# FFN-up products: wide and narrow matmuls alternate singly, with the narrow product of the low weights ahead of the wide product of the high weights

## The chip, the cores and the metric

The kernel runs on one core of a Trainium2 chip. The metric is the device time of one execution in microseconds. Three timed runs of the kernel before gave 1171.59, 1171.27 and 1169.43 us, so its median is 1171.27 us. The profiled execution, from which all durations below come, took 1171.33 us; its trace spans 1169.3 us from the first to the last instruction. The remaining 2.0 us lie around the span.

## What is computed

The reference is one layer of a decoder trunk on 256 tokens of width 2048: a normalisation, a mixing stage (causal pooling beside an RWKV-7 time mixer) with its output projection, a squared-ReLU feed-forward stage, a gated embedding, and a last normalisation. The feed-forward stage is the one that matters here:

```python
h2 = rms_norm(x, mlp_norm[i])
x = x + jnp.square(jax.nn.relu(h2 @ w_ffn_up[i])) @ w_ffn_down[i]
```

`h2` is 256 x 2048, `w_ffn_up` is 2048 x 8192, `w_ffn_down` is 8192 x 2048, all in float32. The first product, `h2 @ w_ffn_up`, is called FFN-up below, the second FFN-down.

## The kernel before

**Splitting.** Every large product is made of reduced-precision matmuls. Each operand is split into a high part (a rounded copy) and a low part (what the rounding left), and three partial products are added: high by high, low weights by high activations, high weights by low activations. ScalarE writes the high part of the weights (`wh`, L171, two instructions for each block of 1024 columns), VectorE subtracts it from the loaded block to get the low part (`wl`, L172, one instruction). `split_w` does both.

**FFN-up.** `gemm_wide` makes 512 columns of the product at a time, in two halves of 256 columns (each half is one `bank` tile of two PSUM banks, one for each 128 columns, `ct` = 0 and 1). It is called 16 times, so there are 32 halves. A half loads four blocks `raw` of `w_ffn_up`, 128 x 1024 each; a block holds four 128-deep steps `k` of the contraction, 256 columns each. So a half has 16 steps `k`.

Each step `k` is four matmuls, called a *round* below. For both `ct` a **wide** product takes the high weights as the stationary operand and streams 512 columns: the high and the low activations of all 256 tokens side by side (`hl`, two runs of 256). Its first 256 output columns collect high by high, its last 256 high weights by low activations. For both `ct` a **narrow** product takes the low weights and streams the 256 columns of the high activations; it adds into the first 256 output columns of the same bank. Before the change the round is wide, wide, narrow, narrow (L1134 twice, then L1139 twice). There are 32 x 16 = 512 rounds, with 1024 wide and 1024 narrow products.

After the 16th step `consume` is called (`square` in `ffn_half`): ScalarE copies the last 256 columns of both banks out (L1409), VectorE adds the first 256 (L1410), squares the positive part (L1411), and the result is split again for FFN-down. There are two `bank` tiles (pool `psw`), used in turn.

**FFN-down and the rest.** `ffn_half` runs eight calls of `gemm_wide` and then two sweeps over `w_ffn_down` (L1229, 512-column products), and is called twice. So FFN-up has two stretches, about 376 to 556 us and 718 to 896 us. Beside FFN-up, `sums_ahead` prepares sums of `w_ffn_down` blocks (`ta`, L1218 to L1223) on VectorE and writes them to memory.

**What sets the order.** In this part of the kernel no order is written out by hand: a scheduler orders each engine's instructions from the program's text, its priorities (splits of weights have a high one) and the buffers. Loads are issued by SyncE's queue in that order. Loaded blocks have six buffers, high parts five, low parts four. A buffer is free when its last reader is done: the VectorE subtraction for a loaded block, the last wide product of a block for its high part, the last narrow product for its low part.

Of the kernel before, what the change touches and what calls it, by code (L numbers as in the profile page):

```python
# [16 lines left out]
T = 256  # L17
# [23 lines left out]
def trunk(  # L41
# [19 lines left out]
    nc = tc.nc  # L61
# [99 lines left out]
    def load_raw(src, n, name):  # L161
        raw = ring("raw", F32, f"raw_{name}")
        nc.sync.dma_start(raw[:, 0:n], src)
        return raw

    def split_w(raw, name):

        wh, wl = ring("wh", F32R, f"wh_{name}"), ring("wl", F32R, f"wl_{name}")
        with tc.high_priority(20000):
            for a in range(2):  # L170
                nc.scalar.activation(wh[:, a * 512 : (a + 1) * 512], raw[:, a * 512 : (a + 1) * 512], AF.Copy)  # L171
            nc.vector.tensor_tensor(wl, raw, wh.bitcast(F32), op=ALU.subtract)  # L172
        return [(t_h, t_l) for t_h, t_l in zip((wh[:, 0:512], wh[:, 512:1024]), (wl[:, 0:512], wl[:, 512:1024]))]
# [233 lines left out]
    for tt in range(2):  # L407
        for i, q in enumerate((1, 3)):
            nc.tensor.matmul(
                sbank[:, tt : tt + 1], sums[q][:, 0, tt * 128 : (tt + 1) * 128], ones[:, 0:1],  # L410
                start=i == 0 and tt == 0, stop=i == 1, skip_group_check=True,
# [705 lines left out]
    def wide_bank(name):  # L1117
        return psw.tile([128, 2, 512], F32, tag="wide", name=name)

    def gemm_wide(src, acts, name, consume):  # L1120

        for half in range(2):
            bank = wide_bank(f"{name}_w{half}")
            for kq in range(4):
                raw = load_raw(src[half, kq].rearrange("p a n -> p (a n)"), 1024, f"{name}{half}_{kq}")
                for a, (wh, wl) in enumerate(split_w(raw, f"{name}{half}_{kq}")):
                    for b in range(2):
                        k = kq * 4 + 2 * a + b  # L1130
                        hl = acts(k)
                        cs = [slice(b * 256 + ct * 128, b * 256 + ct * 128 + 128) for ct in range(2)]
                        for ct, c in enumerate(cs):
                            nc.tensor.matmul(  # L1134
                                bank[:, ct, :].rearrange("p (s t) -> p s t", s=2), wh[:, c], hl,
                                start=k == 0, stop=False, skip_group_check=True,
                            )
                        for ct, c in enumerate(cs):
                            nc.tensor.matmul(  # L1139
                                bank[:, ct, 0:T], wl[:, c], hl[:, 0, :], start=False, stop=k == 15, skip_group_check=True  # L1140
                            )
            consume(half, bank)

# [257 lines left out]
    def ffn_half(hf):  # L1401
        acts = []
        for i in range(8):
            f = hf * 8 + i

            def square(bi, bank):
                r = fp.tile([128, 512], F32, tag="r", name=f"r{f}_{bi}")
                r2 = r.rearrange("p (c t) -> p c t", c=2)
                nc.scalar.activation(r2, bank[:, :, T : 2 * T], AF.Copy)  # L1409
                nc.vector.tensor_tensor(r2, bank[:, :, 0:T], r2, op=ALU.add)  # L1410
                nc.vector.scalar_tensor_tensor(r, r, 0.0, r, op0=ALU.max, op1=ALU.mult)  # L1411
                pr = i * 2 + bi
                if pr in SEVEN:
                    acts.append(square_seven(r, pr))
                else:
                    acts.append(square_plain(r, pr))

            gemm_wide(w_up[f], h2, f"u{f}", square)
            if f == 1:
                inv_ms()  # L1420
                x_store(1)
            sums_ahead(hf, i // 4, AHEAD[i % 4])

        for j in range(2):
            np_ = (hf + j) % 2
            hooks = {3: lambda: (x_store(1 - np_), x_load(3, np_))} if j else {}
            if hf and j:
                hooks[max(AHEAD) + 1] = lambda: (x_load(4, 1), ps_.extend(split_p()))
            sweep(w_down[:, hf * 16 : hf * 16 + 16], acts, hf, np_, f"d{hf}{np_}", scaled_residual, hooks)
# [163 lines left out]
```

## Time and profile before

| what | value |
|---|---|
| median of three timed runs | 1171.27 us |
| profiled execution | 1171.33 us |
| its span | 1169.3 us |
| FFN-up, two stretches | about 376 to 556 us, 718 to 896 us |
| wide products (L1134) | 1024, recorded at 395 ns on average |
| narrow products (L1139) | 1024, recorded at 278 ns on average |
| low parts of FFN-up weights (L172, `wl_u`) | 128, 1221 ns each |
| high parts of FFN-up weights (L171, `wh_u`) | 256, 624 ns each |

PE stands for the matmuls of TensorE, PEld for its loads of stationary operands, DVE for VectorE, ACT for ScalarE, SP for the queue that issues the loads. A row of a group gives its line, engine, operation, the tile written and the tiles read, the shapes, the number of instructions, then the busy time in us, the mean ns of one, and the time for which the engine was idle just before them with what ended it. Matmuls overlap: the recorded duration of one is longer than the distance to the start of the next, and that distance, called the *pitch* here, is what the time is made of.

### The profile page before, as it was taken

Reading aid. Unit: us, or ns where it says so; the run is one execution under the profiler, and the core shown is the slowest. Engines: PE = TensorE matmul, PEld = TensorE weight load, DVE = VectorE, ACT = ScalarE, POOL = GpSimd, SP = SyncE. Lnnn points to the kernel's source line nnn. Section 1 sums busy time; section 2 is a strip of 40 time slices with the busy share of each in tenths; the row PEclk is TensorE's granted clock in tenths of the full one; section 3 lists DMA queues with packets and bytes.
Section 4 is the critical chain, followed back from the end, with each engine's and each line's share of the span. In section 5 each row is a group of like instructions: output and inputs, shape, how many; then the busy total and the mean of one; then the engine's idle time right before and its main releaser. Section 6 shows DMA issues by size and latency. Waiting matters only on the chain.

```text
span 1169.3 us, 19239 instructions
## 1 busy us (share of the span) xinstructions
PE 1155.1 (99%) x7360; PEld 992.7 (85%) x7360; DVE 904.5 (77%) x1193; ACT 685.9 (59%) x1216; POOL 18.3 (2%) x77
## 2 busy tenths in 40 slices
PE   9999999999999999999999999999999999999997
PEld 8999998787888888888888888888888888888886
DVE  7886898356555787887989988777878899898843
ACT  5868555666545555554764664554555664659733
POOL 4100000000000000000000000000000000000000
PEclk9999999999999999999999999999999999999998
DMA  7554444444756888788677867887986777886812
GB/s 272 163 171 129 156 154 146 138 152 127 233 183 207 303 294 302 260 288 291 219 272 237 304 243 233 302 292 261 323 300 229 264 274 258 292 292 219 302 55 72
DMA packets 73547, 269.36 MB, mean 230 GB/s; under 512 B 8176, under 2 KB 9200, under 8 KB 70512
## 3 DMA queue, kind: packets, MB, share of 16 engines
q1 hardware_dynamic: 73168, 267.78, 66.4%
q8 instruction: 57, 0.93, 0.3%
q10 hardware_dynamic: 288, 0.37, 0.1%
q14 instruction: 34, 0.28, 0.1%
HBM read 246.09 MB, written 22.02 MB: 229 GB/s over the span
## 4 chain that ended last, share of the span: by engine, by line
PE 95%; ACT 2%; DVE 2%; DMA 1%; issue 0%; SPq 0%; DVEq 0%; ACTq 0%
PE u_w L1134 20%; PE d_p L1229 16%; PE u_w L1139 10%; PE d_w L1229 8%; PE d_d L1229 3%; PE o_b L193 2%; PE o_b L194 2%; PE o_b L195 2%; PE gt_b L195 2%; PE gt_b L194 2%; PE gt_b L193 2%; PE zr_b L184 1%; PE zk_b L184 1%; PE zk_b L185 1%; PE zr_b L185 1%; PE zk_b L186 1%
## 5 line engine op out<-in xcount | busy, mean ns | idle before, releaser
L1134 PE MATMUL u_w<-h,wh_u 128*128 128x512 f32 x1024 | 321.7, 395 | 0.0
L171 ACT ACTIVATE wh_u<-raw_u 128x512 fp32r<-128x512 f32 x256 | 147.3, 624 | 152.6 <-PE u_w L1134 94.7
L1139 PEld LDWEIGHTS u_w<-h,wl_u 128*128 128x128 f32 x1024 | 192.3, 188 | 45.3
L1139 PE MATMUL u_w<-h,wl_u 128*128 128x256 f32 x1024 | 201.5, 278 | 0.0
L172 DVE TENSOR_TENSOR wl_u<-raw_u,wh_u 128x1024 fp32r<-128x1024 f32 x128 | 156.1, 1221 | 45.5 <-PE u_w L1139 34.9
L1134 PEld LDWEIGHTS u_w<-h,wh_u 128*128 128x128 f32 x1024 | 156.0, 189 | 0.1
L1229 PE MATMUL d_p<-wh_d,yd 128*128 128x512 f32 x336 | 89.8, 389 | 0.0
L1229 PEld LDWEIGHTS d_p<-wh_d,yd 128*128 128x128 f32 x336 | 62.9, 188 | 12.9
L1291 ACT ACTIVATE th_d<-raw_d 128x1024 fp32r<-128x1024 f32 x40 | 40.3, 1052 | 55.4 <-DVE raw_d L1287 55.4
L171 ACT ACTIVATE wh_d<-raw_d 128x512 fp32r<-128x512 f32 x112 | 63.9, 621 | 9.9 <-ACT th_d L1291 4.8
L172 DVE TENSOR_TENSOR wl_d<-raw_d,wh_d 128x1024 fp32r<-128x1024 f32 x56 | 66.0, 1218 | 0.6 <-PE u_w L1139 0.6
L172 DVE TENSOR_TENSOR wl_o<-raw_o,wh_o 128x1024 fp32r<-128x1024 f32 x32 | 39.1, 1223 | 34.5 <-PE o_b L195 20.6
L171 ACT ACTIVATE wh_o<-raw_o 128x512 fp32r<-128x512 f32 x64 | 36.7, 625 | 39.4 <-PE o_b L194 22.1
L1229 PE MATMUL d_w<-th_d,ys 128*128 128x512 f32 x216 | 55.1, 390 | 0.1
L1293 DVE TENSOR_TENSOR tl_d<-raw_d,th_d 128x1024 fp32r<-128x1024 f32 x40 | 47.3, 1220 | 7.4 <-ACT th_d L1291 7.4
L1229 PE MATMUL d_p<-wl_d,yd 128*128 128x512 f32 x168 | 51.7, 389 | 0.0
L1280 ACT ACTIVATE w7h_d<-raw_d 128x1024 fp32r<-128x1024 f32 x36 | 38.0, 1060 | 22.1 <-PE d_d L1229 11.2
L1293 DVE TENSOR_TENSOR tl_d<-tr_d,th_d 128x1024 fp32r<-128x1024 f32 x32 | 37.8, 1221 | 13.9 <-ACT th_d L1291 13.9
L1229 PEld LDWEIGHTS d_w<-th_d,ys 128*128 128x128 f32 x216 | 40.4, 188 | 9.1 <-ACT th_d L1291 0.8
L1282 DVE TENSOR_TENSOR w7l_d<-raw_d,w7h_d 128x1024 fp32r<-128x1024 f32 x36 | 43.9, 1218 | 3.3 <-PE u_w L1139 1.6
L1229 PE MATMUL d_p<-w7h_d,ys 128*128 128x512 f32 x144 | 44.3, 389 | 0.0
L1291 ACT ACTIVATE th_d<-tr_d 128x1024 fp32r<-128x1024 f32 x32 | 32.2, 1052 | 11.8 <-PE d_p L1229 11.7
(393 smaller groups left out, 2650.1 us busy)
## 6 DMA issues: line engine op xcount, KB each, us to landing
raw_u<-in_w_ffn_up_dram SPq DMA_DIRECT2D x128, 512.0 KB, 5.9
raw_d<-in_w_ffn_down_dram SPq DMA_DIRECT2D x112, 512.0 KB, 5.0
raw_o<-in_w_out_dram SPq DMA_DIRECT2D x32, 512.0 KB, 3.6
raw_ta<-in_w_ffn_down_dram SPq DMA_DIRECT2D x32, 512.0 KB, 4.3
tad<-ta SPq DMA_DIRECT2D x16, 1024.0 KB, 5.8
tr_d<-tad SPq DMA_DIRECT2D x32, 512.0 KB, 5.1
raw_gt<-in_w_ple_gate_dram SPq DMA_DIRECT2D x24, 512.0 KB, 4.5
raw_zk<-in_w_in_dram SPq DMA_DIRECT2D x16, 512.0 KB, 3.5
```

What stands on the lines that cost most here:

```text
L171: nc.scalar.activation(wh[:, a * 512 : (a + 1) * 512], raw[:, a * 512 : (a + 1) * 512], AF.Copy)
L172: nc.vector.tensor_tensor(wl, raw, wh.bitcast(F32), op=ALU.subtract)
L193: nc.tensor.matmul(o, a_h, wh[:, 0:n], start=first, stop=False)
L194: nc.tensor.matmul(o, a_l, wh[:, 0:n], start=False, stop=False)
L195: nc.tensor.matmul(o, a_h, wl[:, 0:n], start=False, stop=last)
L1134: nc.tensor.matmul(bank[:, ct, :].rearrange("p (s t) -> p s t", s=2), wh[:, c], hl, start=k == 0, stop=False, skip_group_check=True,)
L1139: nc.tensor.matmul(bank[:, ct, 0:T], wl[:, c], hl[:, 0, :], start=False, stop=k == 15, skip_group_check=True)
L1229: nc.tensor.matmul(o, l, r, start=first, stop=last, skip_group_check=True)
L1280: nc.scalar.activation(ha, ra, AF.Copy)
L1282: nc.vector.tensor_tensor(la, ra, ha.bitcast(F32), op=ALU.subtract)
L1291: nc.scalar.activation(th[:, r], tr[r], AF.Copy)
L1293: nc.vector.tensor_tensor(tl[:, r], tr[r], th[:, r].bitcast(F32), op=ALU.subtract)
```

## The change

The four matmuls of a round are written in another order: for each `ct` first the narrow product, then the wide one. The round becomes narrow, wide, narrow, wide. The flag that begins an accumulation (`start`) moves from the wide product to the narrow one, the flag that ends it (`stop`) from the narrow to the wide. Shapes, operands and counts stay.

```diff
-                        cs = [slice(b * 256 + ct * 128, b * 256 + ct * 128 + 128) for ct in range(2)]
-                        for ct, c in enumerate(cs):
+                        for ct in range(2):
+                            c = slice(b * 256 + ct * 128, b * 256 + ct * 128 + 128)
+                            nc.tensor.matmul(
+                                bank[:, ct, 0:T], wl[:, c], hl[:, 0, :], start=k == 0, stop=False, skip_group_check=True
+                            )
                             nc.tensor.matmul(
                                 bank[:, ct, :].rearrange("p (s t) -> p s t", s=2), wh[:, c], hl,
-                                start=k == 0, stop=False, skip_group_check=True,
-                            )
-                        for ct, c in enumerate(cs):
-                            nc.tensor.matmul(
-                                bank[:, ct, 0:T], wl[:, c], hl[:, 0, :], start=False, stop=k == 15, skip_group_check=True
+                                start=False, stop=k == 15, skip_group_check=True,
                             )
```

In the changed kernel the narrow product stands in L1134 and the wide one in L1137; all later lines are one lower.

On PE, the rows where one loaded block (`wh_u_0`, `wl_u_0`) ends and the next (`wh_u_1`, `wl_u_1`) begins, in the middle of the first stretch, were before:

```order
L1134 MATMUL u_w_5523<-h_3764,wh_u_0_5526 128x512 x2
L1139 MATMUL u_w_5523<-h_3764,wl_u_0_5527 128x256 x2
L1134 MATMUL u_w_5523<-h_3764,wh_u_1_5549 128x512 x2
L1139 MATMUL u_w_5523<-h_3764,wl_u_1_5550 128x256 x2
L1134 MATMUL u_w_5523<-h_3764,wh_u_1_5549 128x512 x2
```

and are now:

```order
L1134 MATMUL u_w_5523<-h_3764,wl_u_0_5527 128x256
L1137 MATMUL u_w_5523<-h_3764,wh_u_0_5526 128x512
L1134 MATMUL u_w_5523<-h_3764,wl_u_1_5550 128x256
L1137 MATMUL u_w_5523<-h_3764,wh_u_1_5549 128x512
L1134 MATMUL u_w_5523<-h_3764,wl_u_1_5550 128x256
L1137 MATMUL u_w_5523<-h_3764,wh_u_1_5549 128x512
```

Each block's first product now reads the low part `wl` and its last one the high part `wh`; the other way round before.

The scheduler moves some instructions of the other engines as well. On DVE, the rows around the low part of one block (`wl_u_1_4781`) early in the first stretch, where `ys` and `r` are the splitting and squaring of an earlier half's result, were before:

```order
L177 TENSOR_TENSOR ys_4619<-r_0_4615,ys_4619 128x256
L177 TENSOR_TENSOR ys_4619<-r_0_4615,ys_4619 128x128
L1266 TENSOR_TENSOR r_0_4615<-r_0_4615 128x128
L1267 TENSOR_TENSOR r_0_4615<-r_0_4615 128x128
L1268 TENSOR_TENSOR r_0_4615<-r_0_4615 128x128
L1269 TENSOR_TENSOR r_0_4615<-r_0_4615 128x128
L172 TENSOR_TENSOR wl_u_1_4781<-raw_u_1_4778,wh_u_1_4780 128x1024
L177 TENSOR_TENSOR ys_4619<-r_0_4615,ys_4619 128x512
L172 TENSOR_TENSOR wl_u_2_4804<-raw_u_2_4801,wh_u_2_4803 128x1024
```

and are now:

```order
L177 TENSOR_TENSOR ys_4619<-r_0_4615,ys_4619 128x256
L172 TENSOR_TENSOR wl_u_1_4781<-raw_u_1_4778,wh_u_1_4780 128x1024
L177 TENSOR_TENSOR ys_4619<-r_0_4615,ys_4619 128x128
L1265 TENSOR_TENSOR r_0_4615<-r_0_4615 128x128
L1266 TENSOR_TENSOR r_0_4615<-r_0_4615 128x128
L1267 TENSOR_TENSOR r_0_4615<-r_0_4615 128x128
L1268 TENSOR_TENSOR r_0_4615<-r_0_4615 128x128
L172 TENSOR_TENSOR wl_u_2_4804<-raw_u_2_4801,wh_u_2_4803 128x1024
L177 TENSOR_TENSOR ys_4619<-r_0_4615,ys_4619 128x512
```

The low parts of the weights stand a few instructions earlier, the squaring of finished halves a few later. Moves of this kind recur in both stretches. On SP six loads of `w_ffn_up` blocks move by one to three places:

```order
 L163 DMA raw_u_0_4755<-in_w_ffn_up_dram 128x1024
 L163 DMA raw_u_1_4778<-in_w_ffn_up_dram 128x1024
+L163 DMA raw_u_0_4863<-in_w_ffn_up_dram 128x1024
 L163 DMA raw_u_2_4801<-in_w_ffn_up_dram 128x1024
-L1225 DMA tad_5_4752<-ta_5_4748 128x2048
+L1224 DMA tad_5_4752<-ta_5_4748 128x2048
 L163 DMA raw_u_3_4824<-in_w_ffn_up_dram 128x1024
-L163 DMA raw_u_0_4863<-in_w_ffn_up_dram 128x1024
```

This is the largest of these moves: the load of one block goes ahead of two loads and a store. On ACT three instructions change places with a neighbour. In the sweeps of FFN-down, and everywhere outside FFN-up and its ends, each engine's order is the same as before.

## The prediction

> **What bounds the kernel now.** I read the busy shares first, then the shares of the chain that ended last, then what PE waits for.
>
> ```profile
> PE 1155.1 (99%) x7360; PEld 992.7 (85%) x7360; DVE 904.5 (77%) x1193; ACT 685.9 (59%) x1216; POOL 18.3 (2%) x77
> PE 95%; ACT 2%; DVE 2%; DMA 1%; issue 0%; SPq 0%; DVEq 0%; ACTq 0%
> PE pd L978 <- ACT ybuf L923: 1.6, 1, 1.6
> PE warm_b L349 <- DVE ones L107: 1.1, 1, 1.1
> ...
> PE wag_b L380 <- DMA wag<-in_w_wag_dram: 0.2, 1, 0.2
> ```
>
> PE is busy 99% of the span and makes 95% of the chain. The last three rows are the first two and the last of the eight rows that list what PE's matmuls waited for in the whole run (total us, times, longest); none of the eight names `u_w`, the tile that FFN-up writes. So in FFN-up only the distance from one matmul to the next, the pitch, makes time. The stage by stretches (start and end in us, their length, then busy time and count of PE, PEld, DVE, ACT, POOL, then the granted clock) shows the same:
>
> ```profile
> 384.50:556.00 171.50, 171.50 (x986) 149.60 (x986) 137.52 (x189) 90.19 (x169) 0.00 (x0) 1.00 0.82 290
> 718.00:896.30 178.30, 178.30 (x1026) 155.57 (x1025) 142.28 (x191) 93.71 (x176) 0.00 (x0) 1.00 0.83 290
> L1134 PE MATMUL u_w<-h,wh_u x512: 389/396/398, 717.9 to 895.8; 128*128 128x512 f32 x171
> ```
>
> PE is busy all of both stretches, at a granted clock of 1.00; DVE and ACT are idle a fifth and nearly half of them. The third row is the wide products of the second stretch (min/median/max ns, first and last start). From the first wide to the last, which is the second of its round, lie 255 rounds and one wide of 0.23 us: (177.9 - 0.23) / 255 = **696.7 ns for a round**. Times 512 rounds that is 356.7 us, 30% of the span. Everything the change can do to PE is in this number: 1 ns on a round is 0.51 us.
>
> **The change part by part.** It removes and adds no instruction: 1024 wides, 1024 narrows and as many weight loads before and after, the same bytes. What is new is which product follows which. Before, a round has the neighbours wide-wide, wide-narrow, narrow-narrow, narrow-wide; after, only wide-narrow and narrow-wide, twice. I look at one round of the trace (start in us, recorded us, instruction):
>
> ```profile
> 450.51 0.40 PE L1134 MATMUL u_w<-h,wh_u 128*128 128x512 f32 x1
> 450.75 0.40 PE L1134 MATMUL u_w<-h,wh_u 128*128 128x512 f32 x1
> 450.98 0.28 PE L1139 MATMUL u_w<-h,wl_u 128*128 128x256 f32 x1
> 451.10 0.27 PE L1139 MATMUL u_w<-h,wl_u 128*128 128x256 f32 x1
> 451.21 0.40 PE L1134 MATMUL u_w<-h,wh_u 128*128 128x512 f32 x1
> ```
>
> The pitches are 0.24 (wide, wide next), 0.23 (wide, narrow next), 0.12 (narrow, narrow next), 0.11 (narrow, wide next). The neighbour makes no difference beyond the 0.01 us of the rows. If a product keeps the pitch that it has here with the neighbours that it keeps, two pairs cost 2 x (0.23 + 0.11) to 2 x (0.24 + 0.12), around the 0.697 of the round. For a finer bound I take the same widths where they run among themselves:
>
> ```profile
> 631.36 4.08 PE d_p L1229 x18
> 1159.05 0.28 PE L1491 MATMUL gt3c<-gk,h 128*128 128x256 f32 x1
> ...
> 1160.61 0.28 PE L1492 MATMUL gt3c<-gk,h 128*128 128x256 f32 x1
> L1229 PE MATMUL d_p<-wh_d,yd 128*128 128x512 f32 x336 | 89.8, 389 | 0.0
> L1491 PE MATMUL gt3c<-gk,h 128*128 128x256 f32 x16 | 4.5, 283 | 0.0
> L1134 PE MATMUL u_w<-h,wh_u 128*128 128x512 f32 x1024 | 321.7, 395 | 0.0
> L1139 PE MATMUL u_w<-h,wl_u 128*128 128x256 f32 x1024 | 201.5, 278 | 0.0
> ```
>
> The first row is a piece of the chain in FFN-down: 18 wides in 4.08 us, 226.7 ns each. The next two are narrows of the last stage, 13 apart: 1.56 / 13 = 120 ns each. Two wides and two narrows at these pitches are **693.4 ns**, 3.3 less than the round. The group rows say where the difference sits: a recorded duration is the pitch plus a constant (389 - 226.7 = 162.3, 283 - 120 = 163), so in FFN-up a wide has about 395 - 162.5 = 232.5 ns and a narrow 115.5, 6 more and 4.5 less than among its own.
>
> *The pitch.* The mixture costs 3.3 ns a round. Either it goes with the shares of the widths or the two-run operand of the wide product, and then the order changes nothing: 0. Or it goes with the changes of width, two in a round before and four after, and then it doubles: + 3.3 x 0.51 = **+1.7 us**. Or single alternation settles at the unmixed pitches: **-1.7 us**. No place of this trace alternates singly, so these are bounds; I take **0**, since the nearest row is the round itself, whose two mixed neighbours (0.23 and 0.11) are not longer than its unmixed ones.
>
> *Same bank.* Narrow and wide of one `ct` now follow each other into the same bank, over the same first columns. The narrows of the last stage above add 48 times into one bank, as do the three products of each triple in FFN-down, and keep 120 and 226.7: 0.
>
> *The wait for the low part.* A block's first product now needs `wl`, the later of its two parts, two wides (0.46 us) earlier than before. What is queued behind it is the whole of PE, so the lead decides. It is shortest where the second stretch begins:
>
> ```profile
> 718.78 3.49 DVE L172 TENSOR_TENSOR wl_u<-raw_u,wh_u 128x1024 fp32r<-128x1024 f32 x3
> 717.91 0.62 PE L1134 MATMUL u_w<-h,wh_u 128*128 128x512 f32 x2
> 723.48 0.62 PE L1134 MATMUL u_w<-h,wh_u 128*128 128x512 f32 x2
> 723.94 0.28 PE L1139 MATMUL u_w<-h,wl_u 128*128 128x256 f32 x1
> ```
>
> The stretch starts at 717.91; a block is four rounds, 2.79 us, so its third block starts at 723.48. Its low part is the first of the three of 718.78, done after 1.22 us at 720.00, and first read at 723.94. The lead is 3.9 us, and 3.5 after the change: 0. Without that cover each us of lateness would be one of the end, once for each late block.
>
> *Buffers and queues.*
>
> ```profile
> ACT wh_u L171 <- PE u_w L1134: 94.7, 78, 1.7
> DVE wl_u L172 <- PE u_w L1139: 34.9, 28, 1.6
> ACT wh_u L171 <- DMA raw_u<-in_w_ffn_up_dram: 10.5, 7, 2.3
> 389.54 0.58 ACT L1409 ACTIVATE r<-u_w 128x512 f32<-128x512 f32 x1
> L1410 DVE TENSOR_TENSOR r<-u_w,r x32: 680/691/693, 390.2 to 899.5; 128x512 f32<-128x512 f32 x32
> ```
>
> ACT and DVE wait for PE to free buffers, that is, they run ahead as far as the buffers let them. A high part is now released two narrows (0.23 us) later, a low part one wide (0.23 us) earlier; the lead shrinks by 0.2 of several us. The low parts that the scheduler moved ahead on DVE lengthen it. Six loads change places by up to three; ACT has waited at most 2.3 us for a load without PE noticing: 0. The copy out of a half begins up to two narrows later, since the last wide now ends the half; its bank is needed again one half (11.1 us) later, and 0.23 + 0.6 + 0.7 us are far below that: 0. At the last half before a sweep, the bank is needed after 24 products of 0.227 us, 5.4 us: 0.
>
> The sum is 0 with bounds of -1.7 and +1.7: the profiled execution stays at 1171.3 us, which is the median of the timed runs to 0.1 us.
>
> **The rivals.**
>
> *Slower: single alternation never settles.* In the rows, a wide in this stage has a median of 396 ns, 7 over the settled 389, and a narrow gains 5. If the gain needs a second narrow behind the first, and the loss comes with each wide after a narrow, a pair costs 226.7 + 7 + 120 = 353.7, a round 707.4, 10.7 more: **+5.5 us, 1176.8**. For it: the excess is there only where widths mix. Against it: in the round above the narrow before a wide has the shorter pitch, 0.11. It shows from 2.3 ns on a pair (2.34 us is 0.2%, about the least that a measurement of this kernel can tell from no change).
>
> *Slower: a wait for `wl`.* The lead of 3.5 us would have to vanish, through a load that is held up behind the one that moved ahead of it. Beyond the lead, one block that is late by its own length, 2.79 us, would give **1174.1**, and 2.34 us in all is the point from which it counts. Against it: no row of PE's waits names FFN-up.
>
> *Faster: two narrows in a row are too short for their weight loads.*
>
> ```profile
> L1139 PEld LDWEIGHTS u_w<-h,wl_u 128*128 128x128 f32 x1024 | 192.3, 188 | 45.3
> ```
>
> A load is recorded at 188 ns and a narrow lasts 115.5. If the lateness of the second load is what lengthens the next wides, single narrows, each with a wide behind it, let the wides fall back to 226.7: 2 x (226.7 + 115.5) = 684.4, 12.3 less a round, **-6.3 us, 1165.0**. Against it: the last stage has 96 narrows in a row, each over a load, that hold 120 without growing, so loads recorded at 188 overlap. The Trainium skill (TensorE: Matmul & The Clock Gate, LDWEIGHTS) puts a load at its columns over 1.2 GHz, 107 ns for 128, and lets it run under the product before it. By that rule a load fits under a narrow in either order, and this rival would bring nothing; the pitch of 120 agrees, the recorded 188 alone does not.
>
> *That the change does not do what it says* is ruled out by the order on PE, which is narrow, wide throughout.
>
> **How the numbers follow.** Forecast, within the bounds of 1.7 us: 0.66. Slower by unsettled alternation 0.19, since no row shows single alternation and the excess grows with mixing; by a wait 0.04. Faster 0.11. So faster 0.11, same 0.66, slower 0.23, and 1171.3 us. The range takes in the bounds, on the fast side to 1168.0, where most of the faster case is left out (0.09), on the slow side to 1177.5, just over the first rival's price (0.05 left out).
>
> **What would show it.** In the changed profile, the first and last start of the wides in the second stretch give the round: 696.7 for the forecast, 700 if changes of width cost, about 707 or 684 for the rivals. The group rows show it too, 395 and 278 now. The eight rows of PE's waits must still name no `u_w`. The forecast is wrong if the round moves by more than 4.6 ns, or if PE waits for DVE's `wl_u` or for a load; if the time moves and the round does not, the cause lies at the ends of the stretches.

## The result and the profile after

The changed kernel takes 1174.63 us (median of five timed runs, 1174.61 to 1176.43), the kernel before 1169.54 us beside it (1169.33 to 1171.59). The ratio is 1.0041, with a 95% interval of 1.0030 to 1.0053: 5.1 us slower. Executions of one kernel lie up to 2 us apart, the longer ones mostly at a lower mean granted clock (0.996 or 0.997 for 0.998), so a single time below can be 2 us too long; the two profiled executions (1171.33 and 1176.43 us) are both of the longer kind and differ by 5.1 us as well.

The views that were shown of before, now of the changed kernel: the chain by engine, the two groups of FFN-up, the first and the last of PE's waits, the two stretches by window, and the narrow products of the second stretch with their first and last start.

```profile
PE 94%; DVE 2%; ACT 2%; DMA 1%; issue 0%; SPq 0%; DVEq 0%; ACTq 0%
L1137 PE MATMUL u_w<-h,wh_u 128*128 128x512 f32 x1024 | 362.1, 399 | 0.0
L1134 PE MATMUL u_w<-h,wl_u 128*128 128x256 f32 x1024 | 287.8, 281 | 0.0
PE pd L978 <- ACT ybuf L923: 1.6, 1, 1.6
...
PE pd L978 <- ACT tB_t L923: 0.2, 1, 0.2
384.50:556.00 171.50, 171.50 (x972) 148.69 (x972) 134.78 (x187) 89.94 (x169) 0.00 (x0) 1.00 0.81 285
718.00:896.30 178.30, 178.30 (x1007) 154.59 (x1007) 140.70 (x190) 93.68 (x175) 0.00 (x0) 1.00 0.81 285
L1134 PE MATMUL u_w<-h,wl_u x512: 277/281/284, 720.8 to 901.3; 128*128 128x256 f32 x171
```

PE is as busy as before, at the same granted clock of 1.00, and waits for nothing in FFN-up: none of its eight waits names `u_w`. Yet the same windows hold fewer products, 972 for 986 and 1007 for 1026. From the first narrow to the last lie 511 pairs (a narrow and a wide each), (901.3 - 720.8) / 511 = 353.2 ns each, so a round takes 706.5 ns within 0.4 of rounding; from the starts to the nanosecond in the trace it is **706.7 ns** for 696.6 before. Ten nanoseconds on each of 512 rounds are 5.1 us: the whole difference. A wide is recorded 4 ns longer than before (399 for 395), a narrow 3 ns (281 for 278).

The lead of the low part of the third block in the second stretch, and the waits of ACT and DVE:

```profile
721.64 3.55 DVE L172 TENSOR_TENSOR wl_u<-raw_u,wh_u 128x1024 fp32r<-128x1024 f32 x3
726.42 0.28 PE L1134 MATMUL u_w<-h,wl_u 128*128 128x256 f32 x1
ACT wh_u L171 <- PE u_w L1137: 87.5, 76, 1.7
DVE wl_u L172 <- PE u_w L1134: 16.8, 18, 1.7
ACT wh_u L171 <- DMA raw_u<-in_w_ffn_up_dram: 6.6, 4, 3.1
```

It is subtracted by about 722.9 (721.64 + 1.22) and first read at 726.42, 3.5 us later, as forecast. ACT and DVE still wait for PE to free buffers. Nothing but the pitch moved the time.

### The profile page after: what moved, and what is told of

Same layout as the page of the kernel before. It is cut to its first block, busy times and chain, and to the rows that moved or that the text cites. A ratio compares the mean times of both kernels' runs of the same rounds, so it can differ in the third digit from the quotient of the medians.

```text
span 1174.7 us, 19272 instructions
## 1 busy us (share of the span) xinstructions
PE 1160.4 (99%) x7360; PEld 995.5 (85%) x7360; DVE 904.6 (77%) x1193; ACT 686.7 (58%) x1216; POOL 18.3 (2%) x77
## 4 chain that ended last, share of the span: by engine, by line
PE 94%; DVE 2%; ACT 2%; DMA 1%; issue 0%; SPq 0%; DVEq 0%; ACTq 0%
PE u_w L1137 20%; PE d_p L1228 16%; PE u_w L1134 10%; PE d_w L1228 8%; PE d_d L1228 3%; PE o_b L194 2%; PE o_b L193 2%; PE o_b L195 2%; PE gt_b L193 2%; PE gt_b L195 2%; PE gt_b L194 2%; PE zr_b L184 1%; PE zr_b L185 1%; PE zr_b L186 1%; PE zk_b L184 1%; PE zp_b L193 1%
## 5 line engine op out<-in xcount | busy, mean ns | idle before, releaser
L1137 PE MATMUL u_w<-h,wh_u 128*128 128x512 f32 x1024 | 362.1, 399 | 0.0
L1134 PE MATMUL u_w<-h,wl_u 128*128 128x256 f32 x1024 | 287.8, 281 | 0.0
L1137 PEld LDWEIGHTS u_w<-h,wh_u 128*128 128x128 f32 x1024 | 192.4, 188 | 47.9
L1134 PEld LDWEIGHTS u_w<-h,wl_u 128*128 128x128 f32 x1024 | 193.5, 189 | 0.0
```

Of the source, the lines that this page charges most:

```text
L1134: nc.tensor.matmul(bank[:, ct, 0:T], wl[:, c], hl[:, 0, :], start=k == 0, stop=False, skip_group_check=True)
L1137: nc.tensor.matmul(bank[:, ct, :].rearrange("p (s t) -> p s t", s=2), wh[:, c], hl, start=False, stop=k == 15, skip_group_check=True,)
```

## Theories

Pairs means the order of the kernel before, two wides and then two narrows; singles, or single alternation, means that they take turns one by one. The time of *a* pair, in ns, is that of one wide and one narrow. A: each change between the widths has a price, and singles change twice as often as pairs. B: the narrow product ahead of the wide one is what costs. C: two products in a row into the same bank cost. D: the two-run operand of the wide costs when a narrow stands ahead of it. After the first four runs came E: the alternation has more than one steady rhythm, and what precedes it decides which one holds; with F (the stretch decides) and G (the narrow is too short to hide the weight load behind it) as rivals.

## Experiments

Each was timed against the kernel before on the same chip. Except where said, the work is the same and only the order of the four products of a round differs. W is a wide, N a narrow product. The edits are shown in short: `wide(ct)` and `narrow(ct)` stand for the two matmul calls, `...` for what is left out. Wide first and the runs of four are shown against the round of the kernel before; the one-run layout alone was also tried in the kernel before, and all others change the changed kernel. Halves are counted from 0 to 31 through both stretches, so half 17 is the second of the second stretch. The pitch of a round is worked out from the starts of the matmuls in each trace; rows show it as first and last start and min/median/max of the recorded ns.

### Wide first

```diff
-                        for ct, c in enumerate(cs): wide(ct)
-                        for ct, c in enumerate(cs): narrow(ct)
+                        wide(0); narrow(0); wide(1); narrow(1)
```

> Single alternation with the wide product ahead: wide, narrow, wide, narrow for ct 0, then ct 1, so the high weights are needed first, as before. Theory A (each return to the other width costs, and a run of one pays twice what a run of two does): the round of the second stretch is 706.7 ns as in the changed kernel, time about 5.1 us over the kernel before. Theory B (the narrow product ahead of the wide one is what costs: its wait for the low part, or a narrow followed by a wide into the same bank): the round falls back to 696.7 ns and the time to that of the kernel before.

The time was 1171.45 us for 1169.83 of the kernel before, which is neither the +5.1 us of A nor the 0 of B. The rows for 400 to 550 us (first two) and 740 to 890 us:

```profile
L1136 PE MATMUL u_w<-h,wh_u x434: 391/391/391, 399.7 to 549.8; 128*128 128x512 f32 x145
L1141 PE MATMUL u_w<-h,wl_u x433: 280/280/280, 399.9 to 549.7; 128*128 128x256 f32 x145
...
L1141 PE MATMUL u_w<-h,wl_u x426: 277/281/284, 739.8 to 890.0; 128*128 128x256 f32 x142
L1136 PE MATMUL u_w<-h,wh_u x425: 395/398/403, 739.9 to 889.7; 128*128 128x512 f32 x142
```

In the first stretch all products of a width are alike, and a pair takes (549.8 - 399.7) / 433 = 346.7 ns, a round 693.3: the sum of the pitches that the two widths have among themselves (693.4 in the prediction). In the second, with the same order, three lengths take turns, and a pair takes (889.7 - 739.9) / 424 = 353.3, a round 706.7, as in the changed kernel. A and B both fall: one order has two speeds.

### Another bank, and a one-run operand

The first takes two steps `k` together, so that each narrow is followed by a wide of the other bank; the other two lay the activations out as `[128, NK, 2, T]`, so that the wide streams one run of 512, in the changed kernel and in the kernel before.

```diff
+                    for n_ct in range(2):
+                        for b in range(2):
+                            narrow(ct=n_ct, k=ks[b]); wide(ct=1 - n_ct, k=ks[b])
```

```diff
-        hl = fp.tile([128, 2, NK, T], F32R, tag="h2", name=name)
-        h, l = hl[:, 0], hl[:, 1]
+        hl = fp.tile([128, NK, 2, T], F32R, tag="h2", name=name)
+        h, l = hl[:, :, 0], hl[:, :, 1]
...
-        return part, lambda k: hl[:, :, k, :]
+        return part, lambda k: hl[:, k]
```

> Single alternation in which each narrow product is followed by the wide product of the other ct, so of another bank, and half of the wides are followed by a narrow of another bank (two steps k are taken together: narrow 0, wide 1 for both k, then narrow 1, wide 0 for both). Theory A (width): round 706.7 ns, +5.1 us. Theory C (two products in a row that add into the same columns of the same bank cost): the excess goes with the same-bank neighbours, of which only a quarter is left, so the round is 696.7 to 699 ns, 0 to +1.3 us.

> The changed kernel, with the tile of the activations laid out so that the high and the low activations of a step k lie side by side: the wide product streams one run of 512 columns and not two runs of 256. Theory A (width): round 706.7 ns, +5.1 us. Theory D (the two-run operand makes the wide late when a narrow stands ahead of it): 693.3 to 697 ns, -1.7 to 0 us.

> The kernel before, with the same one-run layout of the activations. Theory A (width): round 696.7 ns, 0 us. Theory D (the two-run operand): 693.3 ns, -1.7 us, the sum of the pitches that the two widths have among themselves.

The wides from 740 to 890 us, in this order:

```profile
L1138 PE MATMUL u_w<-h,wh_u x426: 395/398/403, 739.8 to 889.9; 128*128 128x512 f32 x142
...
L1137 PE MATMUL u_w<-h,wh_u x426: 395/398/403, 739.6 to 889.8; 128*128 128x512 f32 x142
...
L1134 PE MATMUL u_w<-h,wh_u x432: 393/396/398, 739.6 to 889.9; 128*128 128x512 f32 x144
```

The rounds are 706.7, 706.7 and 696.6 ns, the times 1175.69, 1176.10 and 1169.77 us for 1169.83. In the first of the three no narrow is followed by a wide of its own bank, where in the changed kernel each is, and same-bank neighbours are a quarter of all, down from half. (The expectation calls that a quarter of those that there were; it is half of them.) The slow round of 706.7 ns stands all the same, and with a one-run operand too, and pairs do not gain from the latter: C and D fall.

### Six entries

The first step of each half is written in one of six orders, which change from half to half; all other steps are WNWN in the first stretch and NWNW in the second.

```diff
+ first = ("WNWN", "WWNN", "WNWN", "NNWW", "WNWN", "WNNW", "WNWN", "NWWN",
+          "WNWN", "NWNW", "WNWN", "WWNN", "WNWN", "NNWW", "WNWN", "WNNW")
+ seq = first[half_index % 16] if k == 0 else "WNWN" if half_index < 16 else "NWNW"
```

> Single alternation throughout (wide, narrow in the first stretch; narrow, wide in the second), but the first step k of every half is written in one of six orders, which change from half to half. The wide-first run held 693.3 ns a round in all of its first stretch and 706.7 in all of its second. Theory E (single alternation has more than one steady rhythm, and what precedes it decides which one holds): the rounds of a half are 693.3 in some halves and 706.7 in others, and change only behind a first step of another order, in both stretches. Theory A (each change of width costs the same): one pitch everywhere, near 700. Theory F (the stretch decides, by its buffers or its neighbours on the other engines): 693.3 in the first stretch and 706.7 in the second whatever the first step is.

The steady round of each half in ns, from the starts in the trace (halves counted within their stretch):

```
half            0     1     2     3     4     5     6     7     8     9    10    11    12    13    14    15
first step   WNWN  WWNN  WNWN  NNWW  WNWN  WNNW  WNWN  NWWN  WNWN  NWNW  WNWN  WWNN  WNWN  NNWW  WNWN  WNNW
1st stretch 693.3 693.3 693.3 706.7 706.7 706.7 706.7 693.3 693.3 706.7 706.7 693.3 693.3 706.7 706.7 706.7
2nd stretch 706.7 706.7 706.7 706.7 693.3 706.7 706.7 693.3 706.7 706.7 693.3 706.7 706.7 706.7 693.3 706.7
```

Wides of two neighbouring halves of the first stretch (10 and 11; 488.5 to 499 us, 500.5 to 510) and of the second (6 and 7; 786.5 to 796, 798 to 807):

```profile
L1147 PE MATMUL u_w<-h,wh_u 128*128 128x512 f32 x31 | 11.0, 399 | 0.0
...
L1147 PE MATMUL u_w<-h,wh_u 128*128 128x512 f32 x29 | 10.1, 393 | 0.0
...
L1147 PE MATMUL u_w<-h,wh_u 128*128 128x512 f32 x28 | 9.9, 399 | 0.0
...
L1147 PE MATMUL u_w<-h,wh_u 128*128 128x512 f32 x27 | 9.4, 394 | 0.0
```

Both pitches occur in both stretches and with either product first, and no third one. A half keeps its pitch through all its steady rounds; it changes only behind a first step in an order other than the running one, never by itself. Theory E holds, A and F fall. One first step does not always lead to one rhythm: WWNN gives 693.3 twice in the first stretch and 706.7 twice in the second, and within the second stretch alone WNWN gives 693.3 in halves 4, 10 and 14 and 706.7 in halves 0, 2, 6, 8 and 12.

### Longer runs, and a longer narrow

```diff
-                    for b in range(2): wide(0); wide(1); narrow(0); narrow(1)
+                    wide x4 (both b, both ct); narrow x4
```

```diff
-                                bank[:, ct, 0:T], wl[:, c], hl[:, 0, :], start=k == 0, ...
+                                bank[:, ct, 0:384], wl[:, c], hl.rearrange("p s t -> p (s t)")[:, 0:384], start=k == 0, ...
```

> Two steps k are taken together: four wides, then four narrows. Theory A (3.3 ns for each return to the other width): half as many returns, so a round is 693.3 + 1.7 = 695.0 ns, 0.9 us below the kernel before. Theory E (a rhythm that the sequence locks into): no fixed price for a change of width; 693.3 or more, possibly above 696.7.

> The changed kernel with the one-run layout and a narrow product that streams 384 columns: the low weights are also multiplied by the low activations of the first 128 tokens, which adds a small fourth term there. At (columns + 32) / 2.4 ns, which fits 226.7 and 120, a pair would be 226.7 + 173.3 = 400.0 ns and a round 800.0. Theory G (a narrow of 256 is too short to hide the weight load of the wide behind it): with 384 columns the load is hidden, the round is 800.0 and nothing is left of the excess. Theory E (rhythm of unequal widths): an excess may remain, up to the 13.3 ns a round of the changed kernel, 813.

Wides of the runs of four, then narrows and wides of the long narrow (740 to 890 us):

```profile
L1137 PE MATMUL u_w<-h,wh_u x429: 387/396/398, 739.7 to 889.9; 128*128 128x512 f32 x143
...
L1134 PE MATMUL u_w<-h,wl_u x355: 333/337/338, 745.8 to 889.8; 128*128 128x384 f32 x178
L1137 PE MATMUL u_w<-h,wh_u x355: 393/393/395, 746.0 to 889.9; 128*128 128x512 f32 x178
```

Runs of four take (889.9 - 739.7) / 428 = 350.9 ns a pair, 701.8 a round: half as many changes of width, and slower than pairs (1172.56 us for 1169.79). A price per change falls from this side too. The run with 384 columns has the one-run layout as well. A pair takes 144.0 / 354 = 406.8 ns, 6.8 over the 400.0 that the expectation estimates, against 6.7 over 346.7 in the changed kernel; the time was 1228.71 us for the added columns. G falls: 128 more columns above the next load took nothing off the excess, and in the rounds of 693.3 ns the same narrows of 256 columns have no excess to begin with. Whether 400.0 exists behind another first step, or another pitch for runs of four, was not tried.

### Another rhythm by two rounds in 512

The changed kernel, with one first step in each stretch in another order (half 1 and half 17); a control with as many (another order in half 1, and the same order WNWN one half later, in half 18); and the wide-first order with one such step (half 17).

```diff
+ seq = {1: "NWWN", 17: "WNWN"}.get(half_index, "NWNW") if k == 0 else "NWNW"
```

```diff
+ seq = {1: "WNWN", 18: "WNWN"}.get(half_index, "NWNW") if k == 0 else "NWNW"
```

```diff
+ seq = {17: "WWNN"}.get(half_index, "WNWN") if k == 0 else "WNWN"
```

> The changed kernel with 2 of its 512 rounds written in another order: the first step of the second half of each stretch (narrow, wide, wide, narrow in the first stretch; wide, narrow, wide, narrow in the second). These are the orders, and the places in the rhythm, behind which a half of the run with six first steps went from 706.7 to 693.3 ns a round. Theory E (two rhythms, chosen by what precedes): all rounds behind the two are 693.3, about 478 rounds by 13.3 ns = 6.4 us below the changed kernel, 1168.2 to 1168.4 us, so 1.3 us below the kernel before. Theory A or any price per neighbour (two rounds in 512 cannot matter): 5.1 us above the kernel before, as the changed kernel.

> The changed kernel with as many rounds in another order, wide, narrow, wide, narrow in the first step of the second half of the first stretch and of the third half of the second, at places behind which a half of the run with six first steps stayed at 706.7 ns a round. Theory E: 706.7 everywhere, +5.1 us. If any first step of another order brings the faster rhythm, 693.3 behind it.

> The wide-first single alternation, whose first stretch ran at 693.3 ns a round and whose second ran at 706.7, with one round in 512 in another order: the first step of the second half of the second stretch is wide, wide, narrow, narrow. Theory E: 693.3 in all rounds but the 16 ahead of it, 3.2 us below the wide-first run, about 1.4 us below the kernel before. Theory A or F: as the wide-first run, 1.6 us above the kernel before.

Wides of the first of them, called relocked below, from 400 to 550 and from 740 to 890 us, of the control from 740 to 890, and of the wide-first one in both windows:

```profile
L1144 PE MATMUL u_w<-h,wh_u x434: 392/394/395, 399.9 to 550.0; 128*128 128x512 f32 x145
...
L1144 PE MATMUL u_w<-h,wh_u x434: 392/394/395, 739.8 to 890.0; 128*128 128x512 f32 x145
...
L1144 PE MATMUL u_w<-h,wh_u x426: 387/398/403, 739.7 to 889.9; 128*128 128x512 f32 x142
...
L1144 PE MATMUL u_w<-h,wh_u x426: 395/398/403, 399.8 to 550.0; 128*128 128x512 f32 x142
...
L1144 PE MATMUL u_w<-h,wh_u x434: 392/394/395, 739.7 to 889.8; 128*128 128x512 f32 x145
```

In the relocked kernel every steady round behind the two steps takes 693.3 ns, in both stretches; in the control 706.7 stands (1174.40 us). Two rounds of 512, all with the same products, take the 5 us away: this shows that the rhythm, not the order itself, is what the changed kernel pays for.

The starts also show what parts the relocked kernel from its control in the second stretch, where both cut in with WNWN. The wides of the slow rhythm take 241, 236 and 233 ns to the next start in turn. In the relocked kernel the step stands behind a wide of 241 ns, in the control behind one of 233. From each start to the next in ns, with a bar where half 17 of the relocked kernel (first row) and half 18 of the control begin:

```
W241 N120 W236 N113 W233 N117 W241 | W238 N116 W230 N117 N118 W233 N117 W231
W233 N117 W241 N120 W236 N113 W233 | W235 N116 W224 N118 N120 W233 N118 W241
```

In these two runs and the one with six entries, WNWN cuts into a slow narrow-first rhythm at nine places: the four behind a wide of 240 or 241 ns went to 693.3, the five behind one of 232 to 235 ns stayed at 706.7. So the place in the cycle at which the step comes decides, and not the step alone.

Eleven timed executions of the relocked kernel gave a median of 1169.71 us (1168.19 to 1170.87) for 1169.76 before, ratio 0.9994 (0.9985 to 1.0002). Those at a clock of 0.998 took 1168.2 to 1168.7 us, with one at 1170.1, where the kernel before took 1169.5 to 1170.1; the expected 1.3 us less is likely but not clear of noise.

The wide-first kernel did as expected in the second stretch, 693.3 behind its step, but its first stretch now ran at 706.7, and eleven executions gave 1171.76 us (1171.34 to 1173.65), ratio 1.0016 (1.0007 to 1.0025). That asked for the next run.

### The same program again, and pairs with other entries

> The wide-first single alternation a second time, now timed in eleven or so executions. Its first stretch held 693.3 ns a round in the one profile so far, while the same order held 706.7 there in the profile of the relocked kernel. If the program fixes the rhythm, all executions lie near the 1171.5 us of the first time (1.6 us over the kernel before). If the start of the first stretch, where matmuls wait for VectorE, decides anew in each execution, some lie near 1171.5 and others 3.3 us higher, near 1174.8.

> The order of the kernel before (wide, wide, narrow, narrow) in all steps but the first of each half, which takes the six orders in turn as in the run with single alternation. If pairs have one rhythm only, each half runs at 696.7 ns a round behind its first step. If they too have several, some halves run at another steady pitch, 693.3 the lowest that the unmixed pitches allow.

The wide-first kernel unchanged, timed eleven times: 1171.01, 1171.27, 1171.39, 1171.49, 1171.87; 1173.27, 1173.35, 1173.53; 1174.51, 1174.94, 1175.10 us. The first five and the last three have clocks of 0.998 and 0.999, 3.4 us between their means, and 256 rounds by 13.3 ns are 3.4 as well; the middle three have 0.997. All eleven are of one chip, so the chip does not decide between them. Its profile this time (1174.94 us), wides from 400 to 550 us, and below it the pairs from 740 to 890:

```profile
L1136 PE MATMUL u_w<-h,wh_u x425: 395/398/403, 399.9 to 549.7; 128*128 128x512 f32 x142
...
L1147 PE MATMUL u_w<-h,wh_u x432: 387/396/403, 739.8 to 890.0; 128*128 128x512 f32 x144
```

The very program whose first stretch ran at 391/391/391 runs it here at 395/398/403. So the rhythm of the first stretch is decided anew in each execution. In both traces the stretch begins among transposes of the activations (L1158), one of whose loads waits 0.5 us for VectorE, and the first wide takes 314 ns in one and 319 in the other. Both then run in the slow rhythm for eight pairs, up to four more transposes. These come behind a wide of 240 ns in the first trace, and the round is 693.3 from there on; they come behind one of 233 in the second, and 706.7 stays. The place in the cycle thus parts these two as well.

Pairs, behind all six first steps, came back to 696.7 ns within two or three rounds in each of the 32 halves: no entry that was tried gives them another rhythm (1171.62 us at a clock of 0.996).

## Why the prediction went as it did

The range held the time; the likeliest case, no change, did not come, and the first rival's size did.

*What bounds the kernel* was right: only the pitch of FFN-up moved, and 1 ns on a round was 0.51 us.

*The pitch* is the step of the prediction that failed. It took 0, with bounds of -1.7 and +1.7, on the premise that a product keeps the pitch that it has beside a given neighbour. The round went up by 10.0 ns, 5.1 us. The runs show no price per neighbour: NWNW takes 693.3 or 706.7 ns with the same neighbours throughout, pairs 696.7, runs of four 701.8. The lower bound was a real state, reached in the relocked kernel; the upper bound had no ground, since it doubled a price per change of width, which the runs of four contradict.

*The first rival* (707.4 ns, +5.5 us, 1176.8) had the size within 0.7 ns a round: 706.7, +5.1, 1176.4 in the profiled execution. Its mechanism, that a single alternation never settles, was half right. The excess does stay, but as a settled rhythm beside a faster one, and not because a narrow lacks a second narrow behind it, since single narrows reach 693.3 too. That the size came so near is luck: the rival put 7 ns on a wide and nothing on a narrow, and by the starts a wide took 9.9 ns more than among its own (236.6 for 226.7) and a narrow 3.3 less (116.7 for 120). Its chance, 0.19, was too small: the argument against it leaned on one pitch of 0.11 us in a round of pairs, which says nothing of singles.

*Same bank*, *the wait for the low part*, *buffers and queues* were right at 0: the run with another bank keeps the round, the lead is 3.5 us as worked out, and none of PE's waits names `u_w`.

*The faster rival* gave 684.4 ns, which no run reached; 693.3 is the lowest of all. It let the wides fall back to 226.7 and the narrows keep 115.5; in the fastest rhythm, the first stretch of wide first, they take 230.0 and 116.7. The rule of the Trainium skill beside it (TensorE: Matmul & The Clock Gate, LDWEIGHTS), that a load of 128 columns takes about 107 ns and lies under the product before it, is in line with the run of 384 columns (6.8 ns of excess for 6.7): more cover for the load changed nothing.

*The range* was wide enough only because it took in the rival's price; the bounds of the forecast itself, 1.7 us either way, did not hold 5.1.

What stays open is what the rhythm hangs on inside TensorE. Banks, the runs of the operand, the order of the two, the stretch and the length of the narrow are not it. That a step behind the longest wide of the slow cycle switches it is read off the traces; why it does is not shown, and for first steps other than WNWN the places are too few to tell. Narrow first started slow in both stretches of every trace that has it (the changed kernel, other bank, one-run layout, and up to the altered steps the relocked kernel and its control); whether it can start fast is not known.

## What to carry to other kernels

Where TensorE is busy throughout and matmuls of unequal widths mix, do not add up prices per neighbour, which failed here: measure the steady pitch of the exact sequence, and look at min/median/max of a group, which tell one rhythm from another at a glance. Prefer an order that falls back to one pitch whatever precedes it, as the pairs here do, over one that is faster in one rhythm and slower in another. When a change of order moves the time by one or two per cent of its stage (5.1 of 356.7 us here), disturb a single round before explaining the order.

## What was not expected

The same sequence of matmuls, with no wait and at a granted clock of 1.00, holds 693.3 or 706.7 ns a round for 170 to 180 us on end, and one round in another order can switch it. The same program can take either from one execution to the next, 1171.0 to 1171.9 or 1174.5 to 1175.1 us. Among steady states, a pair of widths 512 and 256 reached 346.7 ns, which is the sum of the two alone, so mixing need not cost anything.
